# Turning the GLA values in 32x32 blocks on VectorE instead of transposing them on TensorE

## The chip, the cores and the metric

The kernel runs on one core of a Trainium2 chip. The metric is the device time of one execution in microseconds (us). Three runs of the kernel before took 1454.15, 1454.77 and 1455.24 us; the median is 1454.77. Everything in the profile is from one further execution under the profiler.

TensorE (PE in the profile) does the matmuls and transposes into PSUM, VectorE (DVE) and ScalarE (ACT) do elementwise work, GpSimd (POOL) does small copies and starts the stores, SyncE (SP) starts the loads.

## The reference

One layer of a decoder trunk runs for a prompt of 1024 tokens and for 8 sample rows. From the normalised input one combined projection makes all branch inputs. Three branches follow: gated linear attention (GLA, 4 heads, key dimension 128, value dimension 256), causal pooling, and cross-attention into 256 memory tokens. Each branch is gated and projected, the three are summed, and an output projection with a residual and a last norm ends it.

The change touches the GLA values. In chunked form the GLA computes, per head and chunk, with `q_dec`, `k_inv` and `k_end` being queries and keys scaled by cumulated forget gates:

```
att     = where(tril, q_dec @ k_inv.T, 0)
o_intra = att @ v                  # contracts over tokens
dS      = k_end.T @ v              # contracts over tokens
o       = o_intra + q_dec @ S_before
S       = decay * S + dS
```

`v` is the slice of the combined projection for the head, 1024 tokens by 256 columns. Both products with `v` contract over tokens, and TensorE contracts over partitions, so both need `v` with tokens on partitions.

## The kernel before, in words

Everything is float32. Each large product is made of three matmuls (`mm3`, lines 240 to 242): an operand is split into a high part on ACT (line 221) and a remainder on DVE (line 222), and hi*hi + hi*lo + lo*hi is summed in PSUM.

The combined projection is cut into 40 pairs of 256 output columns (class `Pair`). A pair is computed in seven half-size products by a Strassen scheme, each in two column halves of 258 (`run_product`). Channels lie on partitions and tokens on the free axis: a pair's result is a set of 128 channels by 512 tokens (and 4 sample columns) tiles. The pairs come in the order cross-attention queries (4), GLA queries (2), keys (2), values (4), pooling inputs (4), merge gates (12), branch gates (12). A pair ends in two halves: after its fifth product `finish(p.e1, 0)` and after its seventh `finish(p.e2, 1)` copy the sample columns on POOL (line 565) and store the half to a DRAM scratch tile with one DMA on POOL's queue (line 574). For the values the scratch is `v_scr4`, one tile per head, with channels on partitions.

Between the products a stream of other work is emitted in small steps: first cross-attention (`cross_steps`), then GLA (`gla_steps`), then pooling (`pool_steps`). `fill` is called after each half product and takes steps in proportion to their costs in the `yield` statements. GLA begins when cross-attention is through. For each of 16 (head, chunk) units, chunks having 256 tokens, it loads gates, keys and queries two units ahead and values one unit ahead, and does two blocks of 128 tokens: `gla_within` makes the masked attention block and the transposes of `k_end` and of `v` into one PSUM tile `pz` and splits all 512 columns of it; `gla_recur`, a few steps later, multiplies them and updates the state. `gla_out` turns the normalised outputs back.

The order of the instructions on TensorE and on SP is the order in the program (`manual_schedule`); on ACT, DVE and POOL a planner orders them at build time by priorities. Weights are prepared `AHEAD = 3` products ahead of TensorE (`prepare`), and their loads go through SP's queue, in order with the loads of the other streams. SBUF buffers come from tags with fixed counts: `R` gives one of 14 buffers of 512 columns (tag `ring`) that cross-attention, GLA and pooling share; `V` one of 4, `RAW` one of 3 for weights, `PZ` one of 2 PSUM tiles for the streams, `PX` one of 6 for the products. A buffer is given again once all readers of its tile are through.

In cross-attention the sample rows have their own steps (`cross_sample`): the memory values `vc` are loaded straight into the matmuls of line 796, four loads of 256 KB for each half of the rows.

Of the kernel before, what the change touches and what calls it, by code (L numbers as in the profile page):

```python
# [10 lines left out]
F32R = mybir.dt.float32r  # L11
# [7 lines left out]
P = 128  # L19
# [5 lines left out]
NH = 4  # L25
# [22 lines left out]
def trunk_kernel(ctx: ExitStack, tc: tile.TileContext,  # L48
# [152 lines left out]
    def scratch(n, name, shape):  # L201
        return [dr.tile(list(shape), F32, name=f"{name}{i}") for i in range(n)]
# [3 lines left out]
    acc_scr = [scratch(NK, f"acc{n}_", (P, TT)) for n in range(2)]  # L206
    mkv_scr = [scratch(NH, f"mkvs{o}", (P, 2, DV)) for o in range(2)]
    al_scr = scratch(2, "als", (P, HT))
    q_scr, k_scr, v_scr4 = (scratch(n, s, PAIR) for n, s in ((2, "qsc"), (2, "ksc"), (4, "vsc")))
    u_scr, xq_raw = (scratch(4, s, PAIR) for s in ("usc", "xqsc"))  # L210
    mix_scr = [scratch(4, f"mixsc{n}_", (P, 2, T)) for n in range(3)]
    m_scr = [scratch(4, f"msc{n}_", PAIR) for n in range(3)]
# [14 lines left out]
    def split_r(src, shape, name, scale=None):  # L227
        hi, lo = R(shape, F32R, name + "h"), R(shape, F32R, name + "l")
        split(hi, lo, src, scale)
        return hi, lo  # L230
# [54 lines left out]
    class Pair:  # L285


        def __init__(self, src, dst, s0=None, gated=None):
            self.src, self.dst, self.s0, self.gated, self.raw = src, dst, s0, gated, [None, None]

        def load(self, i):
            raw = RAW("raw")
# [27 lines left out]
    def cols_of(off):  # L320
        return w_in[:, off:off + 2 * P]

    pairs = []
    for off, dst, s0, n in ((O_XQ, xq_raw, S_XQ, 4), (O_Q, q_scr, S_Q, 2), (O_K, k_scr, S_K, 2),
                            (O_V, v_scr4, S_V, 4), (O_U, u_scr, S_U, 4)):
        pairs += [Pair(cols_of(off + 2 * P * j), dst[j], s0=s0 + 2 * j) for j in range(n)]
    for n in ORDER:
        pairs += [Pair(cols_of(O_M + n * D + 2 * P * j), m_scr[n][j]) for j in range(4)]
    for n, off in ((2, O_XG), (0, O_G), (1, O_PG)):
# [213 lines left out]
    def run_product(n):  # L543

        i, j = seq[n]
        p = pairs[i]

        def saved(acc, c, name):
            r = Q(name)
            nc.scalar.activation(r, acc[c][:, :QT], AF.Copy)  # L550
            return r

        def piece(t, h, c):
            return t[:, h, c * QT:(c + 1) * QT]

        def diagonal(x, e):

            if e == 0:
                return x[:, 0:16].rearrange("p (a b) -> p a b", b=4)[:, 0:4:3]
            return x[:, 4:12].rearrange("p (a b) -> p a b", b=4)  # L560

        def finish(t, e):
            rows = (slice(0, 4, 3), slice(1, 3))[e]
            if p.s0 is not None:
                nc.gpsimd.tensor_copy(diagonal(smp[:, NS * p.s0:], e), t[:, :, 512:HT])
            if p.gated:
                n, g = p.gated
                for i in range(2):
                    ch, hf = divmod((0, 3, 1, 2)[2 * e + i], 2)
                    m = p.mix[e][i]  # L570
                    nc.vector.tensor_tensor(t[:, i, :512], t[:, i, :512], m, op=ALU.mult)
                ss = diagonal(brs[n].rearrange("p k b -> p (k b)")[:, 2 * NS * g:], e)
                nc.vector.tensor_tensor(t[:, :, 512:HT], t[:, :, 512:HT], ss, op=ALU.mult)
            nc.gpsimd.dma_start(out=p.dst[:, rows, :], in_=t)

        def gate(t, h):
            if p.gated:
                act(t[:, h], t[:, h], AF.Silu)

        def mixed(e):  # L580

            if p.gated:
                n, g = p.gated
                for i in range(2):
                    ch, hf = divmod((0, 3, 1, 2)[2 * e + i], 2)
                    p.mix[e].append(loaded(mix_scr[n][g][:, ch, 512 * hf:512 * hf + 512], [512], "mix"))

        if j == 0:
            p.x = [PX() for _ in range(2)]
            p.r1, p.mix = [], ([], [])  # L590
            for c in product(p.x, n, True):
                p.r1.append(saved(p.x, c, "r1"))
                yield
        elif j == 1:
            y = [PX() for _ in range(2)]
            p.e1 = E([2, HT], name="c1")
            for c in product(y, n, True):
                nc.vector.tensor_tensor(piece(p.e1, 0, c), y[c][:, :QT], p.r1[c], op=ALU.add)
                if c:
                    gate(p.e1, 0)  # L600
                yield
        elif j == 2:
            p.r2 = []
            for c in product(p.x, n, False):
                p.r2.append(saved(p.x, c, "r2"))
                yield
        elif j == 3:
            p.z = [PX() for _ in range(2)]
            mixed(0)
            for c in product(p.z, n, True):  # L610
                yield
        elif j == 4:
            for c in product(p.x, n, False):
                r3 = saved(p.x, c, "r3")
                nc.vector.tensor_tensor(piece(p.e1, 1, c), p.z[c][:, :QT], r3, op=ALU.add)  # L615
                if c:
                    gate(p.e1, 1)
                    finish(p.e1, 0)
                yield
        elif j == 5:  # L620
            p.e2 = E([2, HT], name="c2")
            mixed(1)
            for c in product(p.z, n, False):
                nc.vector.tensor_tensor(piece(p.e2, 0, c), p.z[c][:, :QT], p.r2[c], op=ALU.add)
                if c:
                    gate(p.e2, 0)
                yield
        else:
            for c in product(p.x, n, False):
                dst = piece(p.e2, 1, c)  # L630
                if p.gated:
                    act(dst, p.x[c][:, :QT], AF.Silu)
                else:
                    nc.scalar.activation(dst, p.x[c][:, :QT], AF.Copy)
                if c:
                    finish(p.e2, 1)
                yield


    def chunk_of(scr, c):  # L640

        return scr[:, c // 2:4:2, (c % 2) * CT:(c % 2 + 1) * CT]
# [4 lines left out]
    def loaded(src, shape, name, alloc=None):  # L647
        t = (alloc or R)(shape, name=name)
        nc.sync.dma_start(out=t, in_=src)
        return t  # L650
# [266 lines left out]
    def gla_within(h, pr):  # L917

        c, cs = pr // 2, slice((pr % 2) * P, (pr % 2 + 1) * P)
        v = gla["v", h, c]  # L920
        kq, kiqi, _ = gla["g", h, c]
        kt, qd, ki, qi = (x[:, cs] for x in (kq[:, 0], kq[:, 1], kiqi[:, 0], kiqi[:, 1]))
        t = PZ()
        nc.tensor.matmul(t[0:64, 0:P], lhsT=ki[:, 0:64], rhs=qi, start=True, stop=True)  # L924
        nc.tensor.matmul(t[64:P, 0:P], lhsT=ki[:, 64:P], rhs=qd, start=True, stop=True)
        nc.tensor.transpose(t[:, P:2 * P], kt, ident)  # L926
        for i in range(2):
            nc.tensor.transpose(t[:, (2 + i) * P:(3 + i) * P], v[:, i, cs], ident)
        nc.vector.copy_predicated(t[:, 0:P], nmask, zeros)
        gla["w", h, pr] = split_r(t, [512], "akv")  # L930

    def gla_recur(h, pr):
        c, cs = pr // 2, slice((pr % 2) * P, (pr % 2 + 1) * P)
        hi, lo = gla["w", h, pr]
        _, kiqi, decp = gla["g", h, c]
        st = gla.get(("st", h))
        t = PZ()
        td, to = t[:, :DV], t[:, DV:]
        mm3(td, hi[:, P:2 * P], lo[:, P:2 * P], hi[:, 2 * P:], lo[:, 2 * P:], True, True)
        mm3(to, hi[:, :P], lo[:, :P], hi[:, 2 * P:], lo[:, 2 * P:], True, st is None)  # L940
        if st is not None:
            nc.tensor.matmul(to, lhsT=kiqi[:, 1, cs], rhs=st, start=False, stop=True)  # L942
        s2 = wk.tile([P, DV], F32, tag="st", name="st", bufs=2)
        if st is None:
            nc.vector.tensor_copy(s2, td)
        else:
            nc.vector.scalar_tensor_tensor(s2, st, decp[:, pr % 2:pr % 2 + 1], td, op0=ALU.mult, op1=ALU.add)
        gla["st", h] = s2
        if pr == 7:
            nc.gpsimd.dma_start(out=o_gla_p[h], in_=s2)  # L950
        if pr % 2 == 0:
            sq = wk.tile([P, 2], F32, tag="sq", name="sq", bufs=3)
            gla["o", h, c] = R([2, DV], name="on"), sq
        on, sq = gla["o", h, c]
        nc.scalar.activation(on[:, pr % 2], to, AF.Copy)
        nc.scalar.activation(to, to, AF.Square, accum_out=sq[:, pr % 2:pr % 2 + 1])
        if pr % 2:
            r = rstd_of(sq, 1.0 / DV)
            for j in range(2):
                nc.scalar.activation(on[:, j], on[:, j], AF.Copy, scale=r[:, j:j + 1])  # L960

    def gla_values(h, c):
        gla["v", h, c] = loaded(chunk_of(v_scr4[h], c), [2, CT], "v")

    def gla_out(h, c):
        on, _ = gla["o", h, c]
# [81 lines left out]
    def gla_steps():  # L1048
# [7 lines left out]
        for n in range(N + 1):  # L1056
            h, c = divmod(n, 4)
            ph, pc = divmod(n - 1, 4)
            if n + 1 < N:
                gla_gates(*divmod(n + 1, 4))  # L1060
                yield 5
            if n < N:
                gla_within(h, 2 * c)
                yield 2
            if n > 0:
# [478 lines left out]
```

## Time and profile before

| What | Number |
|---|---|
| Runs, median of 3 | 1454.77 us (1454.15 to 1455.24) |
| Profiled execution, first to last instruction | 1455.4 us |
| TensorE busy | 1430.4 us, 98% |
| DVE, ACT, POOL busy | 896.6, 688.4, 159.0 us |
| Granted TensorE clock, mean | 0.998 |
| Moved by DMA | 259.46 MB |

The page gives one number for the profiled execution, its span; no other time of that execution is recorded. In a row of groups stand the line of the kernel, the engine, the operation, output and inputs by their names with partitions and elements, the count, the busy time in all and the mean duration of one in ns, and behind the last bar the idle time of the engine ahead of these instructions with what ended it. PEld is TensorE's weight load, which runs beside the matmuls. A row of one tile's instructions has shortest, median and longest duration in ns and the first and last start. A row of the waits has the total in us, how often and the longest. A row of the timeline or the chain of waits begins with its start and its length in us. A row of a DMA queue has packets, MB and the share of the time of 16 DMA engines.

### The profile page before, as it was taken

What the parts mean: (1) busy time and instruction counts of PE and PEld (TensorE: products, weight loads), DVE (VectorE), ACT (ScalarE), POOL (GpSimd) and SP (SyncE); (2) the same over time, 40 slices, a digit from 0 to 9 for tenths busy, and PEclk for the clock granted to TensorE, in tenths of its full rate; (3) what the DMA queues carried; (4) which work ended last, traced back from release to release, by engine and by line L of the source; (5) the groups of instructions that cost most, each with busy time, mean ns of one, the idle gap of its engine ahead of it and who ended that gap; (6) DMA issues with size and microseconds to landing.
All of it is one profiled execution on the core that took longest, in us unless ns stands there. A gap on an engine that the chain in (4) does not pass through costs nothing.

```text
span 1455.4 us, 28240 instructions
## 1 busy us (share of the span) xinstructions
PE 1430.4 (98%) x10817; PEld 1369.2 (94%) x10817; DVE 896.6 (62%) x2075; ACT 688.4 (47%) x1591; POOL 159.0 (11%) x297
## 2 busy tenths in 40 slices
PE   7999999999999999999999999999999999999998
PEld 6899999999899999999999999999999999999876
DVE  6955756656576767766756668785672443544436
ACT  5744444444565666656554445454472333233312
POOL 3211111111011111111111111110010000000000
PEclk9999999999999999999999999999999999999999
DMA  9345675756445453553544455464595677632633
GB/s 322 127 165 183 204 226 173 227 174 201 158 146 178 149 176 121 166 175 118 180 139 141 153 187 187 147 197 155 191 304 159 219 252 249 231 120 67 230 119 116
DMA packets 181843, 259.46 MB, mean 178 GB/s; under 512 B 20540, under 2 KB 130900, under 8 KB 181700
## 3 DMA queue, kind: packets, MB, share of 16 engines
q1 hardware_dynamic: 159900, 183.87, 40.8%
q0 software_dynamic: 21664, 73.59, 13.3%
q8 instruction: 85, 1.39, 0.4%
q14 instruction: 50, 0.41, 0.1%
q10 hardware_dynamic: 144, 0.20, 0.0%
HBM read 180.47 MB, written 77.59 MB: 177 GB/s over the span
## 4 chain that ended last, share of the span: by engine, by line
PE 87%; DMA 6%; DVE 4%; ACT 1%; issue 1%; SPq 0%; DVEq 0%; POOL 0%; ACTq 0%
PE px L240 25%; PE px L241 24%; PE px L242 24%; PE pz L242 2%; PE pz L240 2%; PE pz L241 2%; DMA qb<-xqs 2%; DMA raw<-in_w_in_dram 1%; DMA vc<-in_cache_mem_v_dram 1%; DVE kc L756 1%; PE pz L942 1%; PE pz L924 1%; DMA wm<-in_w_mv_dram 1%; PE pz L796 1%; PE pz L926 1%
## 5 line engine op out<-in xcount | busy, mean ns | idle before, releaser
L242 PE MATMUL px<-bh,wbl 128*128 128x384 f32 (+1 forms) x576 | 184.1, 320 | 0.0
L241 PE MATMUL px<-bl,wbh 128*128 128x384 f32 (+1 forms) x576 | 184.1, 320 | 0.0
L240 PE MATMUL px<-bh,wbh 128*128 128x384 f32 (+1 forms) x576 | 183.8, 319 | 0.0
L550 ACT ACTIVATE r<-px 128x258 f32<-128x258 f32 x240 | 89.8, 376 | 46.7 <-PE px L242 46.1
L240 PEld LDWEIGHTS px<-bh,wbh 128*128 128x128 f32 x576 | 108.4, 188 | 0.0
L241 PEld LDWEIGHTS px<-bl,wbh 128*128 128x128 f32 x576 | 108.2, 188 | 0.0
L242 PEld LDWEIGHTS px<-bh,wbl 128*128 128x128 f32 x576 | 108.2, 188 | 0.0
L240 PE MATMUL px<-ot,s1h 128*128 128x258 f32 x320 | 93.9, 293 | 0.0
L240 PE MATMUL px<-ot,s3h 128*128 128x258 f32 x320 | 93.4, 292 | 0.0
L240 PE MATMUL px<-o,a12h 128*128 128x258 f32 x320 | 93.3, 291 | 0.0
L240 PE MATMUL px<-o,s4h 128*128 128x258 f32 x320 | 93.0, 291 | 0.2 <-DVE c L615 0.2
L240 PE MATMUL px<-o,a11h 128*128 128x258 f32 x320 | 92.9, 290 | 0.0
L240 PE MATMUL px<-ot,a22h 128*128 128x258 f32 x320 | 92.9, 290 | 0.0
L240 PE MATMUL px<-ot,s2h 128*128 128x258 f32 x320 | 92.3, 288 | 0.0
L241 PE MATMUL px<-o,a11h 128*128 128x258 f32 x320 | 91.0, 284 | 0.3 <-DVE o L222 0.3
L242 PE MATMUL px<-o,a12l 128*128 128x258 f32 x320 | 90.7, 283 | 0.0
L241 PE MATMUL px<-o,a12h 128*128 128x258 f32 x320 | 90.6, 283 | 0.0
L241 PE MATMUL px<-ot,s2h 128*128 128x258 f32 x320 | 90.1, 282 | 0.5 <-DVE ot L222 0.5
L242 PE MATMUL px<-o,a11l 128*128 128x258 f32 x320 | 90.6, 283 | 0.0
L241 PE MATMUL px<-ot,a22h 128*128 128x258 f32 x320 | 90.5, 283 | 0.0
L242 PE MATMUL px<-ot,s3l 128*128 128x258 f32 x320 | 90.4, 283 | 0.0
L241 PE MATMUL px<-ot,s3h 128*128 128x258 f32 x320 | 90.4, 282 | 0.0
(469 smaller groups left out, 4587.3 us busy)
## 6 DMA issues: line engine op xcount, KB each, us to landing
raw<-in_w_in_dram SPq DMA_DIRECT2D x80, 512.0 KB, 3.8
msc<-c POOLq DMA_DIRECT2D x24, 516.0 KB, 4.4
brsc<-c POOLq DMA_DIRECT2D x24, 516.0 KB, 4.0
sig<-msc SPq DMA_DIRECT2D x24, 516.0 KB, 6.0
mix<-mixsc SPq DMA_DIRECT2D x48, 256.0 KB, 4.5
brr<-brsc SPq DMA_DIRECT2D x48, 256.0 KB, 5.3
wbr<-in_w_branch_dram SPq DMA_DIRECT2D x24, 512.0 KB, 5.5
acc<-sig POOLq DMA_DIRECT2D x16, 516.0 KB, 6.1
```

Source lines behind the costliest of these rows:

```text
L240: nc.tensor.matmul(out, lhsT=lh, rhs=rh, start=start, stop=False, skip_group_check=more)
L241: nc.tensor.matmul(out, lhsT=lh, rhs=rl, start=False, stop=False, skip_group_check=more)
L242: nc.tensor.matmul(out, lhsT=ll, rhs=rh, start=False, stop=stop, skip_group_check=more)
L550: nc.scalar.activation(r, acc[c][:, :QT], AF.Copy)
L756: nc.vector.tensor_tensor_reduce(kc[:, a, :], kc[:, a, :], qb[:, bb, :], scale=1.0, scalar=0.0, op0=ALU.mult, op1=ALU.add, accum_out=sc[:, ...
L796: nc.tensor.matmul(t[32 * j:32 * j + 32, :DV], lhsT=pm[:, a, 4 * i + j, :], rhs=vc[j][:, a, :], start=a == 0, stop=a == 1)
L924: nc.tensor.matmul(t[0:64, 0:P], lhsT=ki[:, 0:64], rhs=qi, start=True, stop=True)
L926: nc.tensor.transpose(t[:, P:2 * P], kt, ident)
L942: nc.tensor.matmul(to, lhsT=kiqi[:, 1, cs], rhs=st, start=False, stop=True)
```

## The change

The values are turned when their pair ends, and stored with tokens on rows. `v_scr4` (channels on partitions) is replaced by `vt_scr`, per head a DRAM tile of 1024 tokens by 256 columns. `finish` of a value pair, for each of the two 128x512 tiles of its half, turns each 32x32 block within its own place with one `nc.vector.transpose` into a buffer of `R` and stores it with four DMAs on POOL's queue, one for each 32 channels: 32 partitions (tokens within a block of 32), and in each 16 pieces (the blocks) of 32 channels, which is 128 bytes in DRAM. That is eight DMAs per half, 64 in all, where there were 8. The sample columns of the values aren't stored any more; the copy on line 565, which is what the sample path reads, stays.

`gla_values` loads a chunk as two blocks of 128 tokens by 256 columns, and a new `gla_split` splits it once per chunk into a new buffer (high) and in place (low). `gla_within` loses its two transposes of `v`, and splits 256 columns of `pz` into one buffer in place of 512 into two. `gla_recur` takes the values from the split chunk. Its matmuls are the same in number and shape.

```diff
-    q_scr, k_scr, v_scr4 = (scratch(n, s, PAIR) for n, s in ((2, "qsc"), (2, "ksc"), (4, "vsc")))
+    q_scr, k_scr = (scratch(2, s, PAIR) for s in ("qsc", "ksc"))
+    vt_scr = scratch(NH, "vtsc", (T, DV))
...
         def finish(t, e):
...
+            if p.turned:
+                for i in range(2):
+                    ch, hf = divmod((0, 3, 1, 2)[2 * e + i], 2)
+                    r = R([512], name="vt")
+                    nc.vector.transpose(r, t[:, i, :512])
+                    for q in range(4):
+                        c0 = ch * P + 32 * q
+                        nc.gpsimd.dma_start(out=p.dst[512 * hf:512 * hf + 512, c0:c0 + 32].rearrange("(t r) c -> r t c", r=32),
+                                            in_=r[32 * q:32 * q + 32].rearrange("r (t c) -> r t c", c=32))
+                return
             nc.gpsimd.dma_start(out=p.dst[:, rows, :], in_=t)
...
     def gla_within(h, pr):
...
-        v = gla["v", h, c]
...
         nc.tensor.transpose(t[:, P:2 * P], kt, ident)
-        for i in range(2):
-            nc.tensor.transpose(t[:, (2 + i) * P:(3 + i) * P], v[:, i, cs], ident)
         nc.vector.copy_predicated(t[:, 0:P], nmask, zeros)
-        gla["w", h, pr] = split_r(t, [512], "akv")
+        ak = R([2, DV], F32R, name="ak")
+        split(ak[:, 0], ak[:, 1], t[:, :DV])
+        gla["w", h, pr] = ak[:, 0], ak[:, 1]

     def gla_recur(h, pr):
...
+        vh, vl = (x[:, pr % 2] for x in gla["vs", h, c])
...
-        mm3(td, hi[:, P:2 * P], lo[:, P:2 * P], hi[:, 2 * P:], lo[:, 2 * P:], True, True)
-        mm3(to, hi[:, :P], lo[:, :P], hi[:, 2 * P:], lo[:, 2 * P:], True, st is None)
+        mm3(td, hi[:, P:], lo[:, P:], vh, vl, True, True)
+        mm3(to, hi[:, :P], lo[:, :P], vh, vl, True, st is None)
...
     def gla_values(h, c):
-        gla["v", h, c] = loaded(chunk_of(v_scr4[h], c), [2, CT], "v")
+        gla["v", h, c] = loaded(vt_scr[h][c * CT:(c + 1) * CT].rearrange("(j p) v -> p j v", j=2), [2, DV], "v")
+
+    def gla_split(h, c):
+        gla["vs", h, c] = split_in(gla["v", h, c], [2, DV], "vs")
...
             if n < N:
+                gla_split(h, c)
                 gla_within(h, 2 * c)
```

More of the change, by code (lines that the diff above doesn't have):

```diff
@@ L285, in trunk_kernel, with __init__ @@
     class Pair:
-        def __init__(self, src, dst, s0=None, gated=None):
+        def __init__(self, src, dst, s0=None, gated=None, turned=False):
             self.src, self.dst, self.s0, self.gated, self.raw = src, dst, s0, gated, [None, None]
+            self.turned = turned
         def load(self, i):
@@ L324, in trunk_kernel @@
     for off, dst, s0, n in ((O_XQ, xq_raw, S_XQ, 4), (O_Q, q_scr, S_Q, 2), (O_K, k_scr, S_K, 2),
-                            (O_V, v_scr4, S_V, 4), (O_U, u_scr, S_U, 4)):
-        pairs += [Pair(cols_of(off + 2 * P * j), dst[j], s0=s0 + 2 * j) for j in range(n)]
+                            (O_V, vt_scr, S_V, 4), (O_U, u_scr, S_U, 4)):
+        pairs += [Pair(cols_of(off + 2 * P * j), dst[j], s0=s0 + 2 * j, turned=off == O_V)
+              for j in range(n)]
     for n in ORDER:
```

## The prediction

> **What bounds the kernel now.** I read the busy table of the page first, then the busy time of each engine by stage, then the instructions that touch the tile `v`, then the waits of TensorE, and last the queues.
>
> ```profile
> span 1455.4 us, 28240 instructions
> ...
> PE 1430.4 (98%) x10817; PEld 1369.2 (94%) x10817; DVE 896.6 (62%) x2075; ACT 688.4 (47%) x1591; POOL 159.0 (11%) x297
> ```
> ```profile
> 70.00:389.00 319.00, 311.01 (x2534) 298.43 (x2533) 193.88 (x483) 141.04 (x331) 42.02 (x80) 0.99 0.60 192
> 389.00:776.00 387.00, 385.48 (x3167) 368.25 (x3166) 265.30 (x690) 235.13 (x641) 49.61 (x82) 1.00 0.47 154
> ```
>
> The columns are the stretch, its length, and the busy time of PE, PEld, DVE, ACT and POOL, then granted clock, DMA share and GB/s. The values are projected and stored in the first stretch and a little beyond; the GLA work that uses them lies in the second, where TensorE idles 1.5 us of 387. So there an instruction taken from TensorE shortens the program by the slot that it holds, if nothing new makes TensorE wait. DVE is busy 61% of the first and 69% of the second, ACT 44% and 61%.
>
> **What goes: 64 transposes.** In `gla_within` two transposes of the values per call go, 32 calls.
>
> ```profile
> L928 PE MATMUL pz<-ident,v x64: 272/273/273, 389.9 to 739.3; 128*128 128x128 f32 x64
> ```
> ```profile
> 482.40 0.28 PE L241 MATMUL px<-o,s4h 128*128 128x258 f32 x1
> 482.52 0.29 PE L242 MATMUL px<-o,s4l 128*128 128x258 f32 x1
> ...
> 483.11 0.33 PE L926 MATMUL pz<-ident,kq 128*128 128x128 f32 x1
> 483.27 0.38 PE L928 MATMUL pz<-ident,v 128*128 128x128 f32 x2
> 483.41 0.36 PE L240 MATMUL px<-o,s4h 128*128 128x258 f32 x1
> 483.61 0.28 PE L241 MATMUL px<-o,s4h 128*128 128x258 f32 x1
> ```
> ```profile
> 418.28 0.44 PE pz L971 x4
> ```
>
> The 273 ns is one transpose from entry to end; the next starts long before. What it holds is read from starts: from the first L928 (483.27) to the second product matmul (483.61) are 0.34 us, and one product matmul's step is 0.12 us (the first two rows), so two transposes hold 0.22 us. The chain of waits gives the same for the four transposes of L971: 0.44 us, 0.11 each. 64 x 0.11 = **7.0 us** off TensorE. The longer step behind L926 and L928, 0.20 us from 483.41 to 483.61, stays, because the transpose of `kq` on L926 stays.
>
> A rule bears on this. The Trainium skill, "TensorE: Matmul & The Clock Gate", Part 4 (PE-mode transpose), gives a transpose about 275 ns in a kernel's context, most of it access latency. The row agrees (273 ns), but priced so, 64 would be 17.6 us; latency that overlaps isn't time on the path.
>
> **What moves on ACT and DVE.** The split of the pair's tile covers 256 columns, not 512, and the values are split once per chunk, in SBUF.
>
> ```profile
> L222 DVE TENSOR_TENSOR akvl<-pz,akvh 128x512 fp32r<-128x512 f32 x32 | 22.0, 688 | 6.4 <-ACT akvh L221 5.6
> L221 ACT ACTIVATE akvh<-pz 128x512 fp32r<-128x512 f32 x32 | 18.9, 589 | 9.5 <-DVE pz L929 9.3
> L225 DVE SCALAR_TENSOR_TENSOR xq<-xq,xqsh 128x512 fp32r<-128x512 f32 x16 | 11.0, 685 | 0.0
> L615 DVE TENSOR_TENSOR c<-px,r 128x258 f32<-128x258 f32 x80 | 33.6, 421 | 19.3 <-ACT r L550 19.2
> L550 ACT ACTIVATE r<-px 128x258 f32<-128x258 f32 x240 | 89.8, 376 | 46.7 <-PE px L242 46.1
> L221 ACT ACTIVATE a12h<-raw 128x512 fp32r<-128x512 f32 x40 | 25.2, 629 | 25.1 <-PE px L241 22.3 <-DMA vc<-in_cache_mem_v_dram 1.0 <-ACT r L550 0.6
> L890 DVE TENSOR_TENSOR_SCAN bz<-smask,bz 128x256 f32<-128x256 bf16 x16 | 11.0, 689 | 0.4
> L695 DVE TENSOR_SCALAR p<-p,sm 128x256 f32<-128x256 f32 x32 | 9.9, 350 | 0.5
> ```
>
> DVE: 16 x 0.685 added, 32 x (0.688 - 0.421) = 8.5 saved, so +2.5 us. ACT: 16 x 0.629 = 10.1 added, 32 x (0.589 - 0.376) = 6.8 saved, so +3.3. Both lie in the second stretch, where these engines idle 122 and 152 us; I put them at nothing. The two-matmul chain to `copy_predicated` gets shorter, and a pair's split ends about 0.5 us earlier, which only helps the next `pz` tile.
>
> New on DVE are 16 blockwise transposes of 128x512. The trace has none. Below, an operation with one source: 2 x 0.35 at 256 columns, or 0.7 at most; above, the slowest per column, the scan, 689 ns for 256, so 1.4. I take 0.69, the price of nearly every 512-column row here: 1.4 us per pair half, **11.0 us** in all, within DVE's 125 idle us of the first stretch. If that cover were gone, DVE's 11.0 + 2.5 = 13.5 us would be on the path. At the second half of a pair the transposes also wait for ACT's copy of the last product (L634), which today only POOL waits for; behind them on DVE stand the next evacuation (L598) and splits that are made three products ahead, so TensorE has about 12 us before it notices (a pair of some 27 us, by the stores' times below, has seven products).
>
> **The stores.** Per pair half one store of 516 KB becomes eight of 64 KB, each 32 partitions x 16 pieces of 128 bytes; the sample columns are no longer stored.
>
> ```profile
> L574 POOL DMA_DIRECT2D vsc<-c x8: 554/648/745, 316.0 to 412.0; - x8
> ```
> ```profile
> L278 POOL DMA_DIRECT2D wa<-in_w_in_dram x1: 943/943/943, 5.7 to 5.7; - x1
> ```
> ```profile
> vsc<-c POOLq DMA_DIRECT2D x8, 516.0 KB, 3.9
> ...
> w<-in_w_a_dram POOLq DMA_DIRECT2D x4, 32.0 KB, 6.9
> wa<-in_w_in_dram POOLq DMA_DIRECT2D x1, 64.0 KB, 7.4
> ```
> ```profile
> q1 hardware_dynamic: 15559, 15.78, 41.3%
> q0 software_dynamic: 2089, 7.29, 14.2%
> ```
> ```profile
> DMA packets 604, 0.41 MB, mean 81 GB/s; under 512 B 318, under 2 KB 574, under 8 KB 603
> ...
> q1 hardware_dynamic: 574, 0.28, 25.5%
> ```
>
> POOL first: `wa` is one DMA of 1024 pieces of 64 bytes and takes POOL 0.94 us; a store of 512 pieces lies between that and today's 0.65. Eight are 5.2 to 7.5 us per half instead of 0.65, every 14 us (eight halves from 316.0 to 412.0). What waits behind them on POOL is `mixsc<-xo`, the sample columns, and `vs<-vs` of the first sample; POOL is busy 42 of 319 us, so nothing for TensorE.
>
> Then the DMA engines. The fourth fence is from 300 to 430 us: the POOL queue takes 14.2% x 130 x 16 / 7.29 = 40.5 engine-us per MB, so today's 0.53 MB store takes 21.4 / 16 = 1.34 us of every engine. If only bytes count, the new one takes that too. The last fence is a stretch of 5 us (821 to 826) with 64-byte reads: 25.5% x 5 x 16 = 20.4 us; its 256 pieces of 1 KB at the 55 ns of the stage (41.3% x 130 x 16 / 15559) take 14.1, which leaves 6.3 / 318 = 20 ns for a small one. 4096 pieces over 16 engines at 20 ns are 5.1 us per half. So a half costs an engine **1.3 to 5.1 us**, up to 3.8 more than now. Between them I go by `wa`, the only small pieces on this queue: 1024 of them land 0.5 us later than `w` (2 KB rows, same moment), so 4096 take 2.0 us more.
>
> Who waits for that? The waits of TensorE from 300 to 780 us:
>
> ```profile
> PE pz L796 <- DMA vc<-in_cache_mem_v_dram: 1.9, 2, 1.5
> PE pz L782 <- DVE ps L777: 1.5, 1, 1.5
> PE pz L971 <- ACT on L960: 0.9, 1, 0.9
> PE pz L924 <- DVE akvl L222: 0.5, 1, 0.5
> ```
> ```profile
> 355.58 13.14 SPq L649 DMA_DIRECT2D vc<-in_cache_mem_v_dram  x8
> ```
> ```profile
> 356.54 0.56 POOL L574 DMA_DIRECT2D vsc<-c  x1
> ```
>
> Only the eight loads of `vc` for the last head go straight from a DMA to TensorE with no slack, and a half is stored in their midst. The store adds 2.0 us there: **+2.0 us**. Weights are loaded three products ahead and hide it. The loads of the turned values have the same 256 KB and 1 KB pieces as before. The ring of 14 buffers gains and loses: per chunk one buffer fewer in GLA, two more for some 10 us per half before.
>
> Sum against the profiled execution: 1455.4 - 7.0 + 2.0 = 1450.4. That execution is 0.6 above the median of the runs, so against the median **1449.8 us**.
>
> **The rivals.** (a) *The loads take the gain back, no change.* The stores cost 5.1 us per half and both batches of `vc` end 3.8 us later: 1454.8 - 7.0 + 7.5 = 1455.3, with one batch 1451.6; I call it 1453.5. For it: TensorE already waits 1.9 us there. Against: of eight halves only one meets such loads.
>
> (b) *The stores flood the DMA engines: slower.* Place: the values' four pairs, about 110 us. Without the old stores (8 x 1.34 of 130 us) the engines are 47% busy there, so 58 us are free for 2048 pieces per engine; they are full from 28 ns per piece, and with 12 us of weights in hand and the 7.0 us, the gain is gone from (58 + 12 + 7) / 2048 = 38 ns. At a mean load packet's 55 ns: 113 - 58 - 12 = 43 us late, 1454.8 - 7 + 43 = 1491. For it: no row shows small writes to DRAM. Against: small reads cost 20. The Trainium skill, "DMA: Bandwidth & Descriptors", Specifications, speaks for it: below 512 bytes a DMA engine reads, modifies and writes. Read as twice a small read, an estimate, a piece would take 40 ns, 82 us and so 1459.7; no run here shows such a write.
>
> (c) *DVE becomes what TensorE waits for: slower.* Its 13.5 us come onto the path in the two stretches: 1454.8 - 7.0 + 13.5 = 1461.3. It decides from 7.0 us on. For it: TensorE does wait for DVE at times (1.5 and 0.5 above). Against: those are two waits in 480 us.
>
> (d) *A transpose costs its whole 273 ns*: 64 x 0.273 = 17.5 us, 1437.3. Against it stand the starts.
>
> **How the numbers follow.** Forecast 0.59 (own range 1446 to 1452: all of the 7.0 and today's `vc` wait of 1.9 gone, to 4 us lost); (a) 0.20, (b) 0.09, (c) 0.08, (d) 0.04. 0.2%, about what a measurement of this kernel can tell from no change, is 2.9 us. Faster: forecast and (d), 0.63; same: (a), 0.20; slower: (b) and (c), 0.17. The range goes from 1446 up to (c), 1461, and leaves out (b) and (d).
>
> **What would show it.** No L928 on TensorE, and the step from L926's start to the second product matmul's 0.28 us instead of 0.50; TensorE's busy time in the GLA stretch about 7 us less at the same number of matmuls otherwise; DVE transposes near 0.69 us; POOL's stores at 0.65 to 0.94; the wait of L796 for `vc` grown to about 4 us. I am wrong if that wait or waits for `raw` grow by more than 7 us, if the DMA share from 316 to 425 us goes to 0.9 and more, or if TensorE waits for DVE (`px` buffers, L222) in more than a few places.

## The result and the profile after

| | Median of the runs | Profiled execution | Its span |
|---|---|---|---|
| before | 1454.46 us (1452.89 to 1455.71, 9 runs) | | 1455.4 us |
| after | 1451.43 us (1448.15 to 1453.31, 9 runs) | 1452.08 us | 1450.2 us |

The ratio is 0.9975, with a 95% interval from 0.9966 to 0.9985: 2.2 to 4.9 us less. That is about half of the 7.0 us that the 64 transposes were said to hold. The forecast was 1449.8 us, 1.6 below the median, with a range of 1446 to 1461.

What was to be seen first is there. The page of after:

```profile
span 1450.2 us, 28260 instructions
...
PE 1421.7 (98%) x10753; PEld 1360.2 (94%) x10753; DVE 906.0 (62%) x2107; ACT 689.2 (48%) x1607; POOL 194.9 (13%) x353
```

TensorE has 10817 - 10753 = 64 matmuls fewer. The step behind the transpose that stays (L938) is in after's timeline:

```profile
475.00 0.33 PE L938 MATMUL pz<-ident,kq 128*128 128x128 f32 x1
475.08 0.36 PE L241 MATMUL px<-ot,s3h 128*128 128x258 f32 x1
475.28 0.28 PE L242 MATMUL px<-ot,s3h 128*128 128x258 f32 x1
```

From 475.00 to 475.28 it is 0.28 us, as forecast, where it was 0.50. The new instructions, from after's answer for the tile `vt` (shortest, median, longest in ns, first and last start):

```profile
L584 POOL DMA_DIRECT2D vtsc<-vt x64: 649/649/752, 310.5 to 418.4; - x64
L581 DVE STREAM_TRANSPOSE vt<-c x16: 699/703/711, 309.5 to 413.4; 128x512 f32<-128x512 f32 x16
```

So the DVE transpose was priced right (0.69), and the store on POOL costs no more than a large one (0.65, the low end).

The span fell by 5.2 us, and where is seen when it is cut at the same matmuls in both traces (only the first cut of after lies 0.4 us early). The busy times by stretch, first before, then after (stretch, length, then busy PE, PEld, DVE, ACT, POOL, granted clock, DMA share, GB/s):

```profile
286.60:344.60 58.00, 56.84 (x487) 54.95 (x487) 35.29 (x90) 25.91 (x63) 6.91 (x14) 1.00 0.59 193
344.60:380.30 35.70, 32.26 (x272) 29.54 (x271) 15.83 (x45) 12.59 (x28) 4.24 (x8) 1.00 0.68 212
380.30:781.20 400.90, 399.38 (x3282) 382.10 (x3281) 277.69 (x725) 244.17 (x662) 51.67 (x86) 1.00 0.47 155
```
```profile
283.00:341.00 58.00, 57.17 (x491) 55.28 (x490) 39.31 (x96) 26.34 (x64) 17.18 (x30) 1.00 0.65 191
341.00:381.00 40.00, 32.72 (x271) 29.56 (x271) 18.45 (x50) 12.58 (x28) 16.60 (x27) 1.00 0.68 192
381.00:776.00 395.00, 392.65 (x3218) 375.18 (x3217) 280.64 (x747) 245.28 (x679) 65.26 (x107) 1.00 0.50 157
```

The lengths differ by 0, +4.3 and -5.9 us. The GLA stretch got shorter almost as forecast. But in the 40 us ahead of it TensorE idles 7.3 us where it idled 3.4. The other 3.6 us are a lead that after has ahead of the first turned tile at 309.5 us (3.2 us at 283 us, 3.6 at 297). Up to that tile both programs issue the same instructions in the same order, so that lead is not the change's (the last section has its cause in part).

The waits of TensorE in after, 300 to 780 us:

```profile
PE pz L795 <- DVE ps L790: 2.7, 1, 2.7
PE pz L242 <- DVE pTl L223: 1.8, 1, 1.8
PE pz L809 <- DMA vc<-in_cache_mem_v_dram: 1.7, 1, 1.7
...
PE pz L716 <- ACT xo L728: 1.1, 1, 1.1
```

The wait for `vc`, which was to grow from 1.9 to about 4 us, stayed at 1.7. What grew are waits for DVE and ACT. The chain of waits of after leads back from the longest one; the second fence has the same two loads in before:

```profile
337.91 5.85 DMA qb<-xqs
...
345.39 5.92 DMA qb<-xqs
...
355.68 1.71 DMA raw<-in_w_in_dram
...
360.46 0.69 DVE ws L304
...
361.49 0.33 DVE nm L785
...
362.62 0.35 DVE ps L790
...
363.11 0.26 PE pz L795 x2
```
```profile
341.14 4.86 DMA qb<-xqs
...
347.63 3.73 DMA qb<-xqs
```

`ps` is the softmax of the sample rows' scores of the last head. Its scores are made on DVE from `kc` and `qb`, two rows at a time, and a load of `qb` is asked for only when a buffer of `V` is free, which the rows before free. So two loads stand one behind the other. They took 8.59 us before and 11.77 after: 3.2 us of the 4.3. The rest is in DVE's order. Before, then after:

```profile
353.72 0.42 DVE L756 CUSTOM_DVE_ANT_0 kc<-kc,qb 128x256 f32<-128x256 f32 x1
...
354.41 0.69 DVE L302 TENSOR_TENSOR ws<-raw 128x512 f32<-128x512 f32 x1
...
359.48 0.69 DVE L302 TENSOR_TENSOR ws<-raw 128x512 f32<-128x512 f32 x1 [2.60 <-issue]
...
360.42 0.40 DVE L772 TENSOR_REDUCE nm<-pz 8x1 f32<-8x256 f32 x1
```
```profile
353.68 0.70 DVE L581 STREAM_TRANSPOSE vt<-c 128x512 f32<-128x512 f32 x1
354.31 0.38 DVE L769 CUSTOM_DVE_ANT_0 kc<-kc,qb 128x256 f32<-128x256 f32 x1
...
354.96 0.68 DVE L304 TENSOR_TENSOR ws<-raw 128x512 f32<-128x512 f32 x1
...
360.46 0.69 DVE L304 TENSOR_TENSOR ws<-raw 128x512 f32<-128x512 f32 x1 [3.09 <-issue]
...
361.41 0.40 DVE L785 TENSOR_REDUCE nm<-pz 8x1 f32<-8x256 f32 x1
```

A transpose of 0.7 us stands ahead of the last `kc` product, and with it `ws` starts 0.55 us later. That `ws` frees a weight buffer, and SP asks for the next weights only then (at 355.12 before, 355.68 after). The next `ws` waits for them, and the softmax's `nm` stands behind that `ws` in DVE's order, though it needs nothing from it. With a load of weights that took 4.7 instead of 4.3 us, `nm` starts 1.0 us later than before, counted from the last landing of `qb`. 3.2 + 1.0 = 4.2 of the 4.3 us.

The waits for `pTl` and `xo` hang on the same chain and are not added to it: DVE splits `pTl` behind the `kc` product that waited for the second `qb` (at 351.88 and 351.45 us), and ACT makes `xo` only behind a split of the late `ws`, for which it waited 6.0 us (3.4 before).

### The profile page after: what moved, and what is told of

It is laid out like the page before. It is cut to its first block, busy times and chain, and to the rows that moved or that the text cites. A ratio compares the mean times of both kernels' runs of the same rounds, so it can differ in the third digit from the quotient of the medians.

```text
span 1450.2 us, 28260 instructions
## 1 busy us (share of the span) xinstructions
PE 1421.7 (98%) x10753; PEld 1360.2 (94%) x10753; DVE 906.0 (62%) x2107; ACT 689.2 (48%) x1607; POOL 194.9 (13%) x353
## 4 chain that ended last, share of the span: by engine, by line
PE 86%; DMA 5%; DVE 5%; issue 2%; ACT 1%; SPq 0%; DVEq 0%; POOL 0%; ACTq 0%
PE px L241 25%; PE px L242 24%; PE px L243 24%; DMA qb<-xqs 2%; PE pz L243 2%; PE pz L242 2%; PE pz L241 2%; DMA raw<-in_w_in_dram 2%; DVE kc L769 1%; PE pz L403 1%; PE pz L955 1%; PE pz L936 1%; PE pz L809 1%; PE pz L938 1%; DVE ws L304 0%
## 5 line engine op out<-in xcount | busy, mean ns | idle before, releaser
L241 PE MATMUL px<-ot,s3h 128*128 128x258 f32 x320 | 93.4, 292 | 0.0
L243 PE MATMUL px<-ot,s1l 128*128 128x258 f32 x320 | 90.4, 282 | 0.0
```

The source lines that it names most:

```text
L241: nc.tensor.matmul(out, lhsT=lh, rhs=rh, start=start, stop=False, skip_group_check=more)
L243: nc.tensor.matmul(out, lhsT=ll, rhs=rh, start=False, stop=stop, skip_group_check=more)
```

## The experiments

Where the pieces come from that make DVE late, and whether the gain itself is whole, was asked in three groups of runs. In the tables "against before" is worked out from the ratio: (ratio - 1) x 1454.5 us. In the expectations S, V, P, S2, U and D name the theories that are told in them.

**First group: the two halves of the change, and the price of a transpose.** `e1` stores the halves with one plain DMA and without turning, `e2` turns and stores in large pieces, `e3` stores in small pieces without turning. In all three the values come to stand in the wrong places.

```diff
 # e1
-                for i in range(2):
-                    ch, hf = divmod((0, 3, 1, 2)[2 * e + i], 2)
-                    r = R([512], name="vt")
-                    nc.vector.transpose(r, t[:, i, :512])
-                    for q in range(4):
...
+                nc.gpsimd.dma_start(out=p.dst[512 * e:512 * e + 512].rearrange("(p i y) v -> p i (y v)", i=2, y=2),
+                                    in_=t[:, :, :512])
 # e2
-                    for q in range(4):
...
+                    r0 = 512 * e + 256 * i
+                    nc.gpsimd.dma_start(out=p.dst[r0:r0 + 256].rearrange("(p y) v -> p (y v)", y=2), in_=r)
 # e3
-                    r = R([512], name="vt")
-                    nc.vector.transpose(r, t[:, i, :512])
...
-                                            in_=r[32 * q:32 * q + 32].rearrange("r (t c) -> r t c", c=32))
+                                            in_=t[32 * q:32 * q + 32, i, :512].rearrange("r (t c) -> r t c", c=32))
 # e4: 64 transposes back on TensorE, into columns that nothing reads
         nc.tensor.transpose(t[:, P:2 * P], kt, ident)
+        for i in range(2):
+            nc.tensor.transpose(t[:, (2 + i) * P:(3 + i) * P], kt, ident)
```

> Neither turned nor stored in pieces: a value half goes out with one DMA of 2 KB pieces as before, so the values lie in the wrong places and the GLA result is not the reference's; only the GLA side of the change is left. Theory S (the small-piece stores delay loads in the last sample steps of cross-attention, which costs some 4 us): the whole 7.0 us of the 64 transposes, 1447.5, with TensorE idle between 340 and 380 us at about 3.4 us as before, not 7.3. Rival V (the transposes in DVE's queue cost it): 1447.5 as well. Rival P (a transpose frees only 0.05 us, and nothing is lost elsewhere): 1451.4.

> The 16 transposes on DVE stay, each tile then goes out with one DMA of 128 pieces of 2 KB, so the values lie in the wrong places and the GLA result is not the reference's. Theory S: 1447.5. Rival V: 1451.4, as the change. Rival P: 1451.4.

> No transposes on DVE; the tile itself goes out in the 64 DMAs of 128-byte pieces, so the values are wrong within each 32x32 block. Theory S: 1451.4, as the change, with DVE waiting over 4 us for one load of qb near 350 us. Rival V: 1447.5. Rival P: 1451.4.

> The change with two idle transposes of the keys' tile in each gla_within, into columns of the PSUM tile that nobody reads: the price of 64 transposes by itself, all else as in the change. At 0.11 us each: 1451.4 + 7.0 = 1458.4. Rival P at 0.05: 1454.4. At 0.273 each: 1468.9.

| Kernel | Median | Ratio to before (95%) | Against before |
|---|---|---|---|
| e1, neither | 1446.71 us | 0.9949 (0.9937 to 0.9961) | -7.4 us |
| e2, turned, large pieces | 1449.74 us | 0.9967 (0.9954 to 0.9979) | -4.8 us |
| e3, small pieces, not turned | 1449.39 us | 0.9965 (0.9953 to 0.9977) | -5.1 us |
| after, both | 1451.43 us | 0.9975 (0.9966 to 0.9985) | -3.6 us |
| e4, after and 64 transposes | 1458.81 us | 1.0033 (1.0021 to 1.0045) | +4.8 us |

The gain is whole: e1 has the 7 us, and putting 64 transposes back costs 1458.81 - 1451.43 = 7.4 us by the medians (8.4 by the ratios), 0.115 to 0.13 us each. In the traces e4's GLA stretch is 6.7 us longer than after's, 0.105 each. So the forecast's 0.11 holds, though e4's groups of instructions have each at 273 ns from entry to end:

```profile
L940 PE MATMUL pz<-ident,kq 128*128 128x128 f32 x64 | 12.2, 273 | 0.0
```

Rival (d) falls, and so does P, by which the 7.0 was too much.

S and V each expected one of e2 and e3 at 1447.5 us and the other at 1451.4; both kernels lie in the middle, so neither theory fits alone. That turning costs something without the small pieces, and the small pieces without turning, is likely by this; the times do not show it by themselves, since the intervals of e2 (3.1 to 6.7 us less than before) and e3 (3.3 to 6.8) overlap those of after (2.2 to 4.9) and e1 (5.7 to 9.2).

**Second group: the place.** `e5` computes the values ahead of the GLA queries and keys, so that their halves end elsewhere; `e6` does that to the kernel before. `e7` leaves the pair of head 1, whose halves end beside the last head's sample steps, unturned and stored in one piece; `e8` turns this pair alone (in both the values that are not turned come to stand in the wrong places).

```diff
 # e5 (on after), e6 (on before): order of the first 16 pairs
+    pairs = [pairs[i] for i in (0,1,2,3,8,9,10,11,4,6,5,7,12,13,14,15)]
 # e7; e8 has != in place of ==
+            if p.turned and p.s0 == S_V + 2:
+                nc.gpsimd.dma_start(out=p.dst[512 * e:512 * e + 512].rearrange("(p i y) v -> p i (y v)", i=2, y=2),
+                                    in_=t[:, :, :512])
+                return
             if p.turned:
```

> The change with the four value pairs computed straight after the cross-attention queries, ahead of GLA's queries and keys, so that all turned stores fall between some 195 and 305 us and none near the last head's sample steps (340 to 380 us). Theory S2 (the loss sits in those steps: transposes in DVE's queue and stores in the way of the loads of kc and qb make DVE late, and TensorE with it): the loss of 4.7 us goes, 1447. Rival U (each of the eight halves costs its eighth, wherever it lies): 1451.4, as the change.

> The kernel before with the same order of pairs, so that e5 is not read as the effect of the order alone. Both theories: 1454.5, as before; anything faster is the order's own part in e5.

> The change, but head 1's pair, whose halves are stored at 338 and 355 us, is neither turned nor stored in pieces (its values lie in the wrong places, so its GLA result is not the reference's). Theory S2: 1447. Rival U: a quarter of the loss gone, 1450.2.

> The other way round: only head 1's pair is turned and stored in pieces, the values of heads 0, 2 and 3 go out plainly and lie in the wrong places. Theory S2: 1451. Rival U: a quarter of the loss, 1447.9.

| Kernel | Median | Ratio to before (95%) | Against before |
|---|---|---|---|
| e5, after, values first | 1456.13 us | 1.0010 (1.0001 to 1.0020) | +1.5 us |
| e6, before, values first | 1454.8 us | 1.0007 (0.9996 to 1.0019) | +1.0 us |
| e7, all but head 1 turned | 1449.11 us | 0.9970 (0.9960 to 0.9980) | -4.4 us |
| e8, head 1 alone turned | 1450.78 us | 0.9978 (0.9966 to 0.9991) | -3.2 us |

e8 came out as S2 said: with one pair of four turned, as much is lost as in after (7.4 - 3.2 = 4.2 us against e1, where after has 7.4 - 3.6 = 3.8). e7, where S2 expected the whole gain back, shows no more than 0.8 us of it in the runs. Its trace has the loss at this place gone (table below), but its profiled execution is also its fastest one, 1446.82 us. What the other three pairs cost was not tied to a place. The two do not add up either: against e1, e8 loses 4.2 us and e7 3.0, and after with both 3.8, with intervals of 1.4 to 1.8 us to either side of each; so the runs don't tell how the loss is shared among the pairs.

e5 missed on both sides: against e6 (+1.5 and +1.0 us) the change gains nothing here that the runs can tell. Earlier, the halves meet the sample steps of other heads, and more of them: from 130 to 320 us DVE waits 19.3 us for `qb` in e5 and 14.9 in e6. In e5's trace, in the same stretch:

```profile
PE pz L241 <- DVE pTl L223: 3.6, 2, 3.3
```

That is a wait of the same sort, for the split of cross-attention's softmax on DVE; in e6 it is 0.8 us. What else makes up the rest of e5's loss stays open.

**The chain in eight kernels.** The traces of these runs hold the chain of the section before. The last two `qb` loads, from the chain of waits of e1, e2, e4, e7 and e8:

```profile
340.68 4.84 DMA qb<-xqs
...
347.14 3.72 DMA qb<-xqs
```
```profile
337.87 5.73 DMA qb<-xqs
...
345.23 4.23 DMA qb<-xqs
```
```profile
338.85 5.53 DMA qb<-xqs
...
346.01 4.16 DMA qb<-xqs
```
```profile
339.01 4.97 DMA qb<-xqs
...
345.62 3.17 DMA qb<-xqs
```
```profile
339.59 5.47 DMA qb<-xqs
...
346.69 4.41 DMA qb<-xqs
```

With SP's and DVE's rows of the same stretch they make this table. "To weights" is from the landing of the second `qb` to the issue of the weights (the row of `raw`), "to `nm`" from the issue of the first `qb` to the start of `nm` on DVE. The last three columns are delays against before, all counted from the matmul that before starts at 341.2 us: of the issue of the first `qb`, of TensorE's matmul that waits for `ps` (362.1 us before), and of the matmul that before starts at 380.6 us.

| Kernel | `qb` loads | To weights | To `nm` | First `qb` later | At `ps` later | At 380.6 later |
|---|---|---|---|---|---|---|
| before | 4.86, 3.73 us | 3.76 us | 19.3 us | 0 | 0 | 0 |
| e7 | 4.97, 3.17 | 3.77 | 18.5 | +0.5 | -0.3 | -2.1 |
| e1 | 4.84, 3.72 | 3.77 | 19.7 | 0.0 | +0.4 | -0.8 |
| e3 | 4.9, 4.30 | 3.77 | 19.8 | +1.7 | +2.2 | +0.7 |
| e8 | 5.47, 4.41 | 4.37 | 21.1 | 0.0 | +1.8 | +1.5 |
| e2 | 5.73, 4.23 | 4.36 | 21.4 | +0.1 | +2.2 | +1.2 |
| e4 | 5.53, 4.16 | 4.36 | 21.5 | +1.3 | +3.5 | +2.1 |
| after | 5.85, 5.92 | 4.37 | 23.5 | +0.3 | +4.5 | +4.3 |

In every row the delay at `ps` is the sum of two, to 0.1 us: the first `qb` asked for later, and the longer way from there to `nm` (after: 0.3 + 4.2; e3: 1.7 + 0.5). So the chain accounts for TensorE's delay there in all eight traces. Its steps can be read off:

- Where head 1's pair is turned (e8, e2, e4, after), the weights are asked for 0.60 us later, in each of the four; where it is not, not at all. That is the transpose on DVE.
- In the same four the first `qb` load takes 0.5 to 1.0 us longer, in large pieces (e2) too. So it isn't the size of the pieces. A turned tile is stored by itself, as soon as it is ready, and its store then starts with the load (POOL's rows, after, then before):

```profile
337.91 1.29 POOL L584 DMA_DIRECT2D vtsc<-vt  x2 [8.02 <-DVE vt L581]
```
```profile
344.23 0.72 POOL L574 DMA_DIRECT2D vsc<-c  x1
```

  At 337.91 us SP issues `qb` as well. Before, one store took both tiles of the half and came 3.1 us after the load's issue at 341.14. The early store and the longer load go together in these kernels; that one causes the other is not shown, since no run moves the store alone.
- The second `qb` load takes 4.2 to 4.4 us with e2, e3, e4 and e8, 0.4 to 0.7 more than before, and 5.92 in the profiled execution of after alone. e4 issues the same instructions up to there and took 4.16. So of the 4.2 us that after's way to `nm` is longer, 2.2 are in e4 too, and some 2 are this execution's.
- In e3 and e4 the first `qb` is itself asked for late, since DVE waited 3.0 and 2.7 us for the `qb` load ahead of it (1.3 before). In e3 four small stores start with that load, at 331.27 and 331.29 us. In e4 none does, and after, with the same instructions, waited 1.7: one load differs by a microsecond or two between executions.

Behind `ps` the traces are not alike, so the last column mixes other things in. e1, e2, e3, e4 and e8 have 3.4 us of half clock there (last section), which before, e7 and after don't have. And for `vc` before and after wait 1.9 and 1.7 us, e7 and e8 0.7 and 0.8, the other four not at all. e4 from 340 to 380 us, where after has a clock of 1.00:

```profile
340.00:380.00 40.00, 35.42 (x290) 32.63 (x289) 21.50 (x56) 13.58 (x31) 17.35 (x29) 0.96 0.72 210
```

**Third group: without the sample steps, and two mends.** `e9` and `e10` leave out the last head's loads of `kc` and `qb` and DVE's products, on after and on before. `e11` turns and stores each tile when it is ready, after the second, fifth, sixth and seventh product. `e12` gives `V` a fifth buffer and takes one from the ring.

```diff
 # e9 (on after), e10 (on before), in cross_sample
+        if h == NH - 1:
+            nc.vector.memset(sc, 0.0)
+            fetch = lambda b2: ([], None)
         kcs, qb = fetch(0)
...
-            for bb in range(2):
+            for bb in range(len(kcs)):
 # e11: the loop of finish over i, as turn(t, e, i), is called per tile
                     gate(p.e1, 0)
+                    turn(p.e1, 0, 0)
...
                     finish(p.e1, 0)
+                    turn(p.e1, 0, 1)
...
                     gate(p.e2, 0)
+                    turn(p.e2, 1, 0)
...
                     finish(p.e2, 1)
+                    turn(p.e2, 1, 1)
 # e12
-        return shaped(wk.tile([P, 512], dt, tag="ring", name=name, bufs=NR), shape)
+        return shaped(wk.tile([P, 512], dt, tag="ring", name=name, bufs=NR - 1), shape)
-        return shaped(wk.tile([P, 512], dt, tag="own", name=name, bufs=4), shape)
+        return shaped(wk.tile([P, 512], dt, tag="own", name=name, bufs=5), shape)
```

> The kernel after, with the loads of kc and qb and the DVE products of kc with qb left out for the last head's sample rows (their scores are set to 0, so the sample rows' cross-attention of that head is not computed); everything else stays. The kernel before with the same left out is run beside it. S (the part of the gain that is given back is lost where DVE waits late for qb and kc of the last head, between 341 and 381 us): with that work gone nothing is left to be late, so this kernel is about 7 us below the kernel before with the same cut: 1445 if that one is at 1452. D (turning and storing cost the same wherever they stand: DVE, POOL or the DMA engines are short in general): the difference stays at about 3 us, 1449.

> The kernel before with the same work of the last head's sample rows left out. Its TensorE idles 3.4 us between 340 and 380 us, partly behind the same loads, so it should gain 0 to 3 us: 1452. It is the base for the kernel after with the same cut: 7 us between them by S, 3 by D.

> The kernel after, with each 128x512 tile of a value half turned and stored as soon as it is ready: after the second, fifth, sixth and seventh product instead of two at a time after the fifth and the seventh. The same 16 transposes and 64 stores, in bursts of four. S: a burst holds DVE for 0.7 us in place of 1.4 and the queue of the engines half as long, so part of the 4 us given back returns: 1449, if DVE does not meet other sample steps with them. D: the amount is the same, 1451.4.

> The kernel after, with five buffers for kc, qb and vc in place of four, and 13 in place of 14 in the ring that the streams share (the fifth buffer takes the place of one of these). Now qb of a sample step is asked for only when DVE is through with an earlier kc. S: with a fifth buffer it is asked for a row earlier, DVE's waits for qb shrink from 9 to some 3 us, and some 3 us return: 1448.5, less what the missing ring buffer costs. D: 1451.4, or more by the ring.

| Kernel | Median | Ratio to before (95%) | Against before |
|---|---|---|---|
| e9, after without the last sample steps | 1446.76 us | 0.9946 (0.9930 to 0.9961) | -7.9 us |
| e10, before without them | 1451.65 us | 0.9980 (0.9969 to 0.9991) | -2.9 us |
| e11, tile by tile | 1456.4 us | 1.0005 (0.9994 to 1.0016) | +0.7 us |
| e12, five buffers | 1469.38 us | 1.0101 (1.0084 to 1.0118) | +14.7 us |

e9 is 1451.65 - 1446.76 = 4.9 us below e10: half way between the 7 of S and the 3 of D, so the times alone do not decide. The traces do, for the place: between the same two matmuls e9 loses 0.4 us against e10 (1.36 us ahead at the first, 0.94 at the second), where after lost 4.3. One wait of TensorE is left from 330 to 385 us, for `vc`: 0.9 us in e9, 0.5 in e10.

The spans of e9 and e10 differ by 1453.4 - 1447.8 = 5.6 us. Of the 1.4 us to 7.0, part is in waits for the split of `ak` in the GLA: in e9 1.1 and 0.7 us, in e10 0.3 for its `akvl`.

e11 is worse than after by 0.3%, and both theories had it equal or better. TensorE loses 3.9 us at the place of after's 4.3 (5.5 at `ps`, where after loses 4.5), and the wait for `ps` there is longer:

```profile
PE pz L802 <- DVE ps L797: 3.6, 1, 3.6
```

Against after, e11's trace loses 0.7 us from 302 to 312 us, at its first turned tiles, and 1.6 from 393 us on, in the GLA. By the ratios the kernels differ by 4.3 us, so the larger part of it stays open. Smaller bursts are no mend here.

e12 is 17 us behind after at the matmul that after starts at 297 us, ahead of the first turned tile. The missing ring buffer is the likely cause, though no run has the fifth buffer alone. The turned tiles sit in this ring as well; what they cost by holding its buffers was not tested by itself. Between the two matmuls e12 loses 0.45 us, not 4.3 (at `ps` 1.7, not 4.5). Its first `qb` load takes 6.26 us, longer than after's, and its second is back at

```profile
362.20 4.03 DMA qb<-xqs
```

TensorE is so late by then that the place is no longer quite the same, so this supports the chain and does not prove it. No kernel here that computes everything beats the one after.

## Why the prediction was right, and where it was wrong

**The gain (7.0 us): right.** 0.11 us per transpose from starts; 0.115 to 0.13 from e4's runs, 0.105 from its trace; e1 gains 7.4 us.

**ACT's and DVE's splits (nothing): nearly right.** The split of 256 columns takes DVE and ACT 0.42 and 0.38 us, as taken, and lies beside TensorE; in the GLA of after 1.1 us of waits for `ak` stand where 0.5 of `akvl` stood.

**DVE's transposes: price right, "hidden" wrong at one place.** Each takes 0.70 us. The argument was that DVE is idle 125 us of the stretch and that what stands behind a transpose has 12 us of slack. That is a sum over the stretch and looks only at the weights' splits. At 353.7 us the instruction behind it is the last `kc` product, and then a `ws` which frees the buffer for the next weights, and then `nm`: no slack at all, and 0.6 us show.

**POOL (0.65 to 0.94 us per store): right, at the low end.**

**The DMA engines (1.3 to 5.1 us per half, 2.0 more than before taken): right in size.** The POOL queue from 316 to 425 us (packets, MB, share of 16 engines), before, then after:

```profile
q0 software_dynamic: 1744, 6.07, 14.2%
```
```profile
q0 software_dynamic: 2541, 5.83, 23.1%
```

Before, a MB takes 14.2% x 109 x 16 / 6.07 = 40.8 engine-us. After, the 58 stores of 64 KB in this stretch are 3.8 MB; without the other 2.03 MB at 40.8 they take 403 - 83 = 320 engine-us, 84 per MB, so 2.76 us of each engine per half where it was 1.35. The pieces double a store's cost, and 1.4 us more per half is within the bounds, below the 2.0. Rival (b) falls: the engines are not full.

```profile
316.00:425.00 109.00, 101.07 (x840) 95.49 (x839) 74.41 (x195) 51.94 (x130) 44.53 (x73) 1.00 0.63 169
```

The Trainium skill, "DMA: Bandwidth & Descriptors", Specifications, has an engine read, modify and write below 512 bytes. A doubled cost per byte is in keeping with that, but the estimate of 40 ns per piece made from it is not: 2.76 x 16 / 4096 is 11 ns.

**The `vc` loads (+2.0 us): the step that failed.** It said: "Only the eight loads of `vc` for the last head go straight from a DMA to TensorE with no slack". That was read from TensorE's own waits. Loads that end in a DVE instruction which TensorE waits for later are not in that view. They stood in DVE's waits of before, 340 to 380 us, which the prediction did not read:

```profile
DVE kc L756 <- DMA qb<-xqs: 4.4, 2, 2.2
```

The same wait in after:

```profile
DVE kc L769 <- DMA qb<-xqs: 7.2, 2, 4.4
```

The one for `vc` went from 1.9 to 1.7. TensorE's waits for DVE, which the prediction did list (`ps`, 1.5 us), were the end of this chain. So the loss has its place beside the right neighbours and another way in, and it is larger than 2.0: 3.5 (e4's trace) to 4.5 us (after's) at `ps`, 2.1 and 4.3 at the end of the stretch, and 3.8 between e1 and after by the ratios.

**The sum.** 1449.8 against 1451.43: a gain of 7.4 for 7.0, and some 3.8 given back for 2.0. It stayed within the forecast's own range (1446 to 1452) since that allowed for 4 us of loss. That it came so close is partly luck: the 2.0 us were worked out for a wait that did not grow. Of the rivals, (a) had the kind (late loads take back part of the gain) and not the load, so that its time for one late batch, 1451.6, meets the median by luck as well; (c) had DVE, but two transposes at one place and not 13.5 us of busy time.

Open stays what of the 3.8 us lies outside this place: e7's trace has nothing of the loss there, and its runs are still 3 us above e1's by the ratios. A small part lies in the GLA: between the matmuls that before starts at 380.3 and 781.2 us, e1's trace is 6.6 us shorter than before's, after's 5.9 and e7's 5.8.

## What to carry to other kernels

Busy shares say that an engine has room; they do not say that the instruction behind a new one has. Where an edit adds work to a helper engine or its queue, list for the stretch not only what the bounding engine waits for, but what each helper waits for, and follow those waits on: a load that a helper waits for, and that is asked for only when the helper has freed a buffer, is on the path long before the bounding engine shows it. And a tile that is stored by itself is stored earlier: look at what is loaded at that moment.

## What the runs showed of the hardware that was not expected

**Half the clock for 3.4 us.** In the trace of every kernel here but after, and apart from the last few us, the granted clock is half for one to four stretches of 3.4 us (one is of 6.8), mostly near 124 and 362 us. Before, then after at the same time:

```profile
121.00:124.40 3.40, 1.79 (x13) 1.38 (x11) 2.73 (x5) 2.43 (x5) 0.95 (x2) 1.00 0.68 196
124.50:127.90 3.40, 3.40 (x16) 3.40 (x17) 0.69 (x1) 0.19 (x1) 0.00 (x0) 0.51 0.89 217
```
```profile
124.50:127.90 3.40, 3.27 (x28) 3.06 (x26) 2.46 (x7) 1.94 (x6) 0.00 (x0) 1.00 0.90 304
```

In before it follows a stretch in which TensorE is busy about half the time, and 16 matmuls run in place of 28. Such a stretch costs up to 1.7 us (half of 3.4). Over this one after's lead on before grows from 1.3 to 2.8 us, so it is one part of the 3.6 us by which after was ahead before the change began. It is likely a part of the several us by which runs of one kernel differ, too: the mean clock of after's nine runs lies between 0.996 and 0.999. The Trainium skill, "TensorE: Matmul & The Clock Gate", Part 1, has a free-running window of 3413 ns, after an idle one of which the clock is halved. The length agrees; but the row ahead of it is not idle, it has 1.79 of 3.40 us busy.

**Small pieces are cheap to issue.** A DMA of 512 pieces of 128 bytes takes POOL 0.65 us, as one of 516 KB in large rows did, and the queue's packets rose by 797 in all when 58 such DMAs took the place of 8 large ones, nowhere near 512 for each.
